# Mixer of an encoder block: v stores on the loading queue, one transfer for a q or k tile, earlier splits

## The chip, the cores and the metric

The kernel runs on one core of a Trainium2 chip. The metric is the time of one execution in microseconds (us) on the device; a kernel's time is the median of its runs. The core's engines are PE (TensorE, matrix products), ACT (ScalarE), DVE (VectorE), POOL (GpSimd) and SP (SyncE, which here only issues DMAs). DMAs are issued from the queues of SP (q1 in the profile), ACT (q10) and POOL (q0), and are carried out by the core's 16 DMA engines. Each engine works through its own instructions in order; a DMA issue is such an instruction too, so it waits in its engine's order for what its transfer needs.

## The reference

One layer of an encoder block, all in float32, with a sequence of 1024 tokens (a grid of 16 rows by 64 columns) and a model width of 1024:

```python
h = h + 0.5 * swiglu(rms_norm(h, ffn1_norm), ffn1_w_gate, ffn1_w_up, ffn1_w_down)
u = rms_norm(h, mix_norm)
z = u @ w_in                                  # columns: q | k | v | ssm input | gates
q, k, v, s_in, gates = jnp.split(z, [512, 1024, 1536, 2048], axis=-1)
y_attn = neighbourhood_attention(q, k, v, na_rpb) @ w_attn_out   # 8 heads of 64
y_ssm = s5_branch(s_in, ...) @ w_ssm_out
g_attn, g_ssm = jnp.split(jax.nn.sigmoid(gates), 2, axis=-1)
h = h + (g_attn * y_attn + g_ssm * y_ssm) @ w_out
h = h + 0.5 * swiglu(rms_norm(h, ffn2_norm), ffn2_w_gate, ffn2_w_up, ffn2_w_down)
h = h + (p @ w_ple_proj) * jax.nn.sigmoid(rms_norm(h, ple_norm) @ w_ple_gate)
return rms_norm(h, final_norm)
```

The attention of a token goes over a window of 8 rows by 16 columns around it, with a learned bias. The branch `s5_branch` runs 32 groups of diagonal complex state-space scans in both directions and ends with a gated unit:

```python
y = jax.nn.gelu(y)
y = y * jax.nn.sigmoid(y @ glu_w + glu_b)
```

## The kernel before

**Products.** Every operand of the products is split into a high and a low part of type float32r: `split` (L157 to L160) casts the high part on ACT (L159) and subtracts it on DVE for the low part (L160). `mm3` (L188 to L192) then makes three products: high by high, high by low, low by high. The projections from `u` (`w_in`) to q, k and the gates run as seven half-size products in place of eight (Strassen's scheme), in 128 x 512 blocks: for one pair of output blocks the items 0 to 6 are run by `s_run`; before an item runs, `s_load` has loaded the weight block `blk` (on ACT's queue), `s_prep` has added blocks where the scheme needs it and split the result into `wh` and `wl`, and `s_evac` takes the finished item from PSUM. `s_ahead(n)` loads five items ahead of n and splits one ahead; `s_more(n)` splits all items below n. A banked sum (`px`, `py`) must be copied out (`z`, on ACT) before PE may use its bank again.

**Order.** A generator `mixer_side` makes the work beside the projections: the state-space scans, the attention, and the gated unit. After every few products the main line calls `tick()`, which advances the generator; each `yield n` says how many ticks pass before its next piece. In this way PE's order is written out by hand. The order of ACT, DVE, POOL and SP in this part of the program is decided by a scheduler, which keeps data dependences and the rings of tile buffers.

**Values.** `values(t)` makes v for half of the sequence: 8 blocks by three products into four banks, then for each of 8 quarters a tile `vs` with high and low parts. The store of it to DRAM (`v_d`) is put into the list `later` with the queue that issues it, and `s_store` issues what is in the list. In `values(1)` the first q/k pair's weights are already being prepared. After it the kernel loads the four `s` tiles, from which further operands (`xh`, `xl`) for the projections are made.

**Attention.** 64 units: 8 heads by 4 column blocks (`cb`) by 2 row blocks (`rb`). Unit j makes its scores (`attn_scores`, L1243: `s<-khl,q`), two units later the transposes of the softmax (`attn_turn`, `pt`), another two later the product with v (`attn_values`, `O<-pth,vhl`). Between units PE runs projection products, in the fixed order. K and q lie in DRAM with high and low parts (`k_d` as [4, 2, 128, 1024]: head pair, part, 2 x 64 channels, token; `q_d` as [4, 128, 4, 2, 2, 128]: head pair, 2 x 64 channels, `cb`, then 512 numbers). A k tile holds the high part in partitions 0 to 63 and the low part in 64 to 127; a q tile holds the same 64 rows of `q_d` twice. `load_k` (L1210) is called for the next head in the fourth or sixth unit of a head, `load_q` (L1216) two column blocks ahead. Values are loaded likewise, by one DMA:

```python
vdr = v_d.rearrange("h (r c) d -> h r c d", r=4)
nc.sync.dma_start(hl[0:n].rearrange("p g d -> p (g d)").bitcast(F32), vdr[hd, :, KC0[cb]:KC0[cb] + KNC[cb]])
```

Its source has 4 outer parts, with 24 or 32 runs of 512 numbers in each; its target has 96 or 128 partitions.

**Gated unit.** `glu_load(m)` loads the two halves `yt` of output block m of the scan, `glu_act(m)` applies GELU to them in place on ACT, `glu_raw(k)` loads a weight block `wgs`. `glu_prep(t, k, raws)` splits the weight block into `wgl` and the operand into `yh` and `yl`, in the ring of buffers `tg`. `glu` runs 8 steps of 12 products, with the next step's `glu_prep` issued before each step's products; `part(11)` is the last of the projection pieces before it.

Of the kernel before, what the change touches and what calls it, by code (L numbers as in the profile page):

```python
# [8 lines left out]
F32 = mybir.dt.float32  # L9
F32R = mybir.dt.float32r  # L10
# [8 lines left out]
HT = 512  # L19
# [22 lines left out]
def encoder_block(ctx, tc, I, out):  # L42
# [119 lines left out]
    def ksl(k):  # L162
        return slice(k * P, (k + 1) * P)
# [910 lines left out]
    def part(n):  # L1074

        if "ac" in pools:
            pools.pop("ac").__exit__(None, None, None)
        if n:
            pools["ac"] = tc.tile_pool(name="as", bufs=1, reuse_waits="tile")
            pools["as"], pools["na"] = pools["ac"].__enter__(), n  # L1080
# [129 lines left out]
    def load_k(hd):  # L1210
        hp, i = hd // 2, hd % 2
        t = khl[hd] = ap_.tile([P, SEQ], F32R, tag="k4", bufs=2, name="khl")
        for a, s_ in enumerate(halves2):
            nc.sync.dma_start(t[s_].bitcast(F32), k_d[hp, a, halves2[i]])

    def load_q(hd, cb):  # L1216
        hp, i = hd // 2, hd % 2
        q = qs[hd, cb] = tmp("q", [P, 2, 2, P], F32R)
        for s_ in halves2:
            nc.sync.dma_start(q[s_].rearrange("p a t c -> p (a t c)").bitcast(F32),  # L1220
                              q_d[hp, halves2[i], cb].rearrange("p a t c -> p (a t c)"))

    def load_v(hd, cb):
        n = 4 * KNC[cb]
# [57 lines left out]
    def tg(name, shape=(P, HT), dt=F32):  # L1282
        return pools["as"].tile(list(shape), dt, tag="g", bufs=11, name=name)

    def glu_load(m, new=tmp):
        ygs[m] = [new("yt") for _ in range(2)]
        for i in range(2):
            nc.sync.dma_start(ygs[m][i], y_d[m, :, 4 * i:4 * i + 4].rearrange("p s c -> p (s c)"))
# [11 lines left out]
    def glu_raw(k, new=tg):  # L1300
        raw = new("wgs")
        nc.sync.dma_start(raw, I["wglu"][k])
        return raw

    def glu_prep(t, k, raws):
        w = ap_.tile([P, 2, HT], F32R, tag="k4", bufs=2, name="wgl")
        split(w[:, 0], w[:, 1], raws.pop(0))
        y = tg("yh", dt=F32R), tg("yl", dt=F32R)
        for src, hi, lo in glu_parts(t, k, *y):
            split(hi, lo, src)  # L1310
        if 4 * t + k < 6:
            raws.append(glu_raw((k + 2) % 4))
        return w, y

    def glu(raws):
        steps = [(t, k) for t in range(2) for k in range(4)]
        nxt = glu_prep(0, 0, raws)
        yield 3
        for n, (t, k) in enumerate(steps):
            w, y = nxt  # L1320
            if k == 0:
                os_ = [bank("glu") for _ in range(4)]
            if n in (1, 2):
                glu_act(n + 1)
            if k < 3:
                nxt = glu_prep(*steps[n + 1], raws)
            for m in range(4):
                mm3(os_[m], (w[:, 0, ksl(m)], w[:, 1, ksl(m)]), y, k == 0, k == 3)
            if k == 3:
                for m in range(4):  # L1330
                    sg = tg("sg")
                    A.activation(sg, os_[m], AF.Sigmoid, bias=glub[:, m:m + 1])
                    for src, o in glu_parts(t, m, sg):
                        V.tensor_tensor(o, o, src, ALU.mult)
                    nc.scalar.dma_start(y2_d[t, m], sg)
                    if m == 0 and t == 0:
                        nxt = glu_prep(1, 0, raws)
            yield 2 + k % 2
# [4 lines left out]
    def mixer_side():  # L1343
        yield from u_second()
        while 3 not in stored:
            yield 1
        yield 7
        new_x()
        ld = {}
        for pr in range(3):  # L1350
            ld[pr] = inject_load(pr)
        yield 10
        for pr in range(NPAIR):
            if pr + 3 < NPAIR:
                ld[pr + 3] = inject_load(pr + 3)
            inject(pr, *ld.pop(pr))
            yield 2
        while "v" not in stored:
            scan_steps(1)
            yield 1  # L1360
        part(5)
        for cb in range(4):
            scan_steps(4)
            yield 4
            if cb < 2:
                load_v(0, cb)
        load_tab(0)
        load_tab(1)
        while 0 not in ready:
            scan_steps(1)  # L1370
            yield 1
        units = [(hd, rb, cb) for hd in range(NH) for cb in range(4) for rb in range(2)]
        n = len(units)
        load_k(0)
        load_q(0, 0)
        load_q(0, 1)
        for _ in range(6):
            scan_steps(1)
            yield 2
        sms, pts, O = {}, {}, {}  # L1380
        late.clear()
        lo, so = {}, {}
        for j in range(n + 5):
            if j < n:
                hd, rb, cb = units[j]
                u = j % 8
                if rb == 1 and j // 2 + 2 < 4 * NH:
                    while u == 5 and hd + 1 not in ready:
                        yield 1
                    load_q(*divmod(j // 2 + 2, 4))  # L1390
                if u == 3 and hd + 1 in ready or u == 5 and hd + 1 < NH and hd + 1 not in khl:
                    load_k(hd + 1)
                if j and u in (0, 2, 6):
                    load_tab(3 * (j // 8) + (1, 0, 2, 0, 0, 0, 3)[u])
                sms[j] = attn_scores(hd, rb, cb)
            if 0 <= j - 2 < n:
                pts[j - 2] = attn_turn(units[j - 2][2], sms.pop(j - 2))
            while late:
                nc.scalar.dma_start(*late.pop())
            if 0 <= j - 4 < n:  # L1400
                hd, rb, cb = units[j - 4]
                if rb == 0:
                    O[0] = bank("O")
                attn_values(hd, rb, cb, O[0], pts.pop(j - 4))
                if rb == 0 and (j - 4) // 2 + 2 < 4 * NH:
                    load_v(*divmod((j - 4) // 2 + 2, 4))
            scan_steps(2)
            yield 3 + (j % 8 == 7)
        part(12)
        for p in range(3):  # L1410
            lo[p] = ssm_load(p)
        stored.add("scan")
        scan_steps(NCH)
        yield 4
        raws = []
        for p in range(NPAIR + 1):
            if 3 <= p + 3 < NPAIR:
                lo[p + 3] = ssm_load(p + 3)
            if p < NPAIR:
                so[p] = ssm_out(p, *lo.pop(p))  # L1420
            if p > 0:
                so.pop(p - 1)()
            if p in (6, 10):
                glu_load((p - 6) // 4)
            if p in (10, 14):
                glu_act((p - 10) // 4)
            if p == 11:
                raws.append(glu_raw(0, tmp))
            yield 1 + p % 2
        part(11)  # L1430
        raws.append(glu_raw(1))
        glu_load(2, tg)
        glu_load(3, tg)
        yield from glu(raws)

    start(mixer_side())

# [30 lines left out]
    def values(t):  # L1468
        os_ = [bank("v") for _ in range(4)]
        for k in range(NK):  # L1470
            load_wv()
            if t == 1 and k == 0:
                s_ahead(-2)
            if t == 1 and k == 2:
                s_store()
            if t == 1 and k == 5:
                s_ahead(0)
            wh, wl = Wv[k]
            xs = U[("a11", "a12", "a21", "a22")[2 * t + k // 4]][k % 4]
            for i in range(4):  # L1480
                xh, xl = (x[:, ksl(i)] for x in xs)
                T.matmul(os_[i], lhsT=xh, rhs=wh, start=(k == 0), stop=False)
                T.matmul(os_[i], lhsT=xh, rhs=wl, start=False, stop=False)
                T.matmul(os_[i], lhsT=xl, rhs=wh, start=False, stop=(k == NK - 1))
                tick()
        for i in range(4):
            for q in range(2):
                vs = tmp("vs", [P, 4, 2, 64], F32R)
                ov = os_[i][:, q * 256:(q + 1) * 256].rearrange("p (h d) -> p h d", h=4)
                with tc.high_priority(offset=PRI):  # L1490
                    A.copy(vs[:, :, 0], ov)
                    V.tensor_tensor(vs[:, :, 1], ov, vs[:, :, 0].bitcast(F32), ALU.subtract)
                later.append((nc.scalar, vds[ksl(i % 2), 2 * t + i // 2, 4 * q:4 * q + 4],
                              vs.rearrange("p h a d -> p h (a d)").bitcast(F32)))

    def load_br(t, b):
# [510 lines left out]
```

## Time and profile before

| what | us |
|---|---|
| median of 3 runs (lowest and highest) | 2094.0 (2091.51 to 2095.16) |
| the profiled execution, its own time | 2086.5 |
| its span, first to last instruction | 2084.6 |
| PE busy | 2045.0 |
| DVE busy | 1478.6 |
| ACT busy | 1012.6 |
| POOL busy | 481.2 |
| queue q1 (SP): MB moved; share of 16 DMA engines | 258.13; 39.0% |
| queue q10 (ACT): MB moved; share of 16 DMA engines | 49.32; 7.4% |

All rows but the first are of the profiled execution, which has its own time beside its span. The mixer lies between about 740 and 1200 us of the span. In rows of the profile `L1243` is line 1243 of the kernel; `s<-khl,q` reads "tile s made from tiles khl and q", buffer numbers left out; `x64` is a count. In a row of the timeline the first number is the start and the second the length, and the bracket at its end is the idle time before it and what ended it. In rows of waits the numbers are us in total, number, and longest. A share of 16 DMA engines adds up the time that a queue's packets took, over 16 times the length of the stretch. The mean granted clock of PE is 0.995 of full speed.

### The profile page before, as it was taken

The numbers are of one execution on the slowest core, as the hardware profiler recorded it, in microseconds if no ns is written. First come the engines' busy times: TensorE is split into PE (matmuls) and PEld (weight loads), VectorE is DVE, ScalarE is ACT, GpSimd is POOL, SyncE is SP. The second block draws the span as 40 slices with busy tenths as digits, with TensorE's granted clock in tenths as the row PEclk, the third lists the DMA queues.
The fourth block names the chain that finished last, engine by engine and source line by source line (L and its number), as shares of the span: only waits on it lengthen the run. The fifth ranks groups of instructions, "written<-read, shape, count | busy, mean of one in ns | idle before, by whom it ended". The sixth has DMA issues, their size and how long they took to land.

```text
span 2084.6 us, 27913 instructions
## 1 busy us (share of the span) xinstructions
PE 2045.0 (98%) x9326; PEld 1670.4 (80%) x9326; DVE 1478.6 (71%) x2542; ACT 1012.6 (49%) x1902; POOL 481.2 (23%) x700
## 2 busy tenths in 40 slices
PE   9999999999999999999999999999999999999998
PEld 3788888878888887877887888788888888888887
DVE  7897777667868755777745768986565666786855
ACT  6434333334445434767755646543333334445544
POOL 0037656441000508888331011000000000000000
PEclk9999999999999999999999999999999999999999
DMA  3434444476534466777684875243224238433302
GB/s 133 144 119 147 134 128 127 146 239 194 187 99 135 135 191 205 210 212 219 204 283 160 295 232 120 75 142 126 93 89 138 82 126 294 152 107 93 120 21 81
DMA packets 212592, 319.74 MB, mean 153 GB/s; under 512 B 29536, under 2 KB 79328, under 8 KB 212448
## 3 DMA queue, kind: packets, MB, share of 16 engines
q1 hardware_dynamic: 163216, 258.13, 39.0%
q10 hardware_dynamic: 44112, 49.32, 7.4%
q0 software_dynamic: 5120, 10.51, 2.0%
q8 instruction: 74, 1.21, 0.2%
q14 instruction: 70, 0.57, 0.1%
HBM read 224.01 MB, written 93.85 MB: 152 GB/s over the span
## 4 chain that ended last, share of the span: by engine, by line
PE 52%; DMA 4%; DVE 3%; ACT 2%; issue 1%; SPq 0%; ACTq 0%; DVEq 0%
PE dx L190 2%; PE dx L191 2%; PE dx L192 2%; PE ux L191 2%; PE gx L191 2%; PE ux L190 2%; PE gx L190 2%; PE gx L192 2%; PE ux L192 2%; PE br L192 1%; PE br L191 1%; PE br L190 1%; PE px L190 1%; PE px L192 1%; PE px L191 1%; PE dy L190 1%
## 5 line engine op out<-in xcount | busy, mean ns | idle before, releaser
L159 ACT CAST wh<-hbuf 128x512 fp32r<-128x512 f32 x280 | 172.9, 622 | 389.5 <-PE gx L191 84.7
L160 DVE TENSOR_TENSOR wl<-hbuf,wh 128x512 fp32r<-128x512 f32 x280 | 216.5, 776 | 121.3 <-ACT wh L159 119.2
L159 ACT CAST wh<-wblk 128x512 fp32r<-128x512 f32 x190 | 117.9, 622 | 188.8 <-PE dx L191 82.3
L160 DVE TENSOR_TENSOR wl<-wblk,wh 128x512 fp32r<-128x512 f32 x190 | 130.8, 691 | 50.3 <-ACT wh L159 42.7
L190 PE MATMUL dx<-ah,wh 128*128 128x512 f32 x416 | 163.5, 393 | 0.4 <-DVE hbuf L694 0.3
L192 PE MATMUL dx<-ah,wl 128*128 128x512 f32 x416 | 161.9, 389 | 0.0
L191 PE MATMUL dx<-al,wh 128*128 128x512 f32 x416 | 161.9, 389 | 0.0
L160 DVE TENSOR_TENSOR al<-araw,ah 128x512 fp32r<-128x512 f32 x154 | 106.6, 696 | 51.0 <-PE dx L191 21.1
L190 PE MATMUL gx<-xh,wh 128*128 128x512 f32 x320 | 125.1, 391 | 1.5 <-DVE c L581 1.5
L190 PE MATMUL ux<-xh,wh 128*128 128x512 f32 x320 | 125.1, 391 | 0.4 <-DVE c L581 0.4
L191 PE MATMUL gx<-xl,wh 128*128 128x512 f32 x320 | 124.5, 389 | 0.0
L192 PE MATMUL ux<-xh,wl 128*128 128x512 f32 x320 | 124.5, 389 | 0.0
L192 PE MATMUL gx<-xh,wl 128*128 128x512 f32 x320 | 124.5, 389 | 0.0
L191 PE MATMUL ux<-xl,wh 128*128 128x512 f32 x320 | 124.5, 389 | 0.0
L159 ACT CAST ah<-araw 128x512 fp32r<-128x512 f32 x154 | 95.0, 619 | 46.4 <-PE dx L191 14.2
L1167 POOL TENSOR_TENSOR sc<-X,rho 128x128 f32<-128x128 f32 x128 | 82.5, 645 | 59.5 <-ACT X L1150 49.6
L160 DVE TENSOR_TENSOR wl<-blk,wh 128x512 fp32r<-128x512 f32 x84 | 61.5, 732 | 46.9 <-ACT wh L159 43.6
L190 PEld LDWEIGHTS dx<-ah,wh 128*128 128x128 f32 x416 | 78.1, 188 | 18.6 <-DVE hbuf L694 1.2
L428 DVE TENSOR_TENSOR hbuf<-hbuf 128x512 f32<-128x512 f32 x120 | 90.3, 753 | 3.1 <-DMA hbuf<-in_wu 1.0
L191 PEld LDWEIGHTS dx<-al,wh 128*128 128x128 f32 x416 | 78.1, 188 | 16.7 <-issue 0.7
L192 PEld LDWEIGHTS dx<-ah,wl 128*128 128x128 f32 x416 | 78.1, 188 | 16.4
L190 PE MATMUL dy<-ah,wh 128*128 128x512 f32 x208 | 80.9, 389 | 0.0
(395 smaller groups left out, 5684.4 us busy)
## 6 DMA issues: line engine op xcount, KB each, us to landing
araw<-a_d SPq DMA_DIRECT2D x154, 256.0 KB
a_d<-c SPq DMA_DIRECT2D x148, 256.0 KB
wblk<-in_wd SPq DMA_DIRECT2D x88, 256.0 KB
hbuf<-in_wg SPq DMA_DIRECT2D x40, 512.0 KB
hbuf<-in_wu SPq DMA_DIRECT2D x40, 512.0 KB
blk<-in_win ACTq DMA_DIRECT2D x48, 256.0 KB
hbuf<-in_xT SPq DMA_DIRECT2D x32, 256.0 KB
h_d<-hbuf ACTq DMA_DIRECT2D x32, 256.0 KB
```

Of the source, the lines that this page charges most:

```text
L159: A.copy(hi, src)
L160: return eng.tensor_tensor(lo, src, hi.bitcast(F32), ALU.subtract)
L190: T.matmul(o, lhsT=wh, rhs=xh, start=first, stop=False, skip_group_check=more)
L191: T.matmul(o, lhsT=wh, rhs=xl, start=False, stop=False, skip_group_check=more)
L192: T.matmul(o, lhsT=wl, rhs=xh, start=False, stop=last, skip_group_check=more)
L428: V.tensor_tensor(b11, (b12, b22, None, None, b21)[i - 2], b11, ALU.subtract)
L1167: G.tensor_tensor(sc, both, rho4, ALU.mult)
```

## The change

- A k tile is loaded by one DMA to 128 partitions instead of two to 64; so is a q tile, whose source is read twice by a broadcast.
- The 16 stores of `v_d` are issued by SP's queue instead of ACT's.
- In `values(1)`, at its sixth block, the first q/k pair's items 1 and 2 are split as well (`s_more(2)`).
- The first `glu_prep` is made ahead of `part(11)`, in another ring of buffers (`tmp`); the loads behind it come in another order, and `glu` gives two ticks, not three, before its first products.

```diff
--- before.py
+++ after.py
@@ -1210,15 +1210,14 @@
     def load_k(hd):
         hp, i = hd // 2, hd % 2
         t = khl[hd] = ap_.tile([P, SEQ], F32R, tag="k4", bufs=2, name="khl")
-        for a, s_ in enumerate(halves2):
-            nc.sync.dma_start(t[s_].bitcast(F32), k_d[hp, a, halves2[i]])
+        nc.sync.dma_start(t.bitcast(F32), k_d[hp, :, halves2[i]])
 
     def load_q(hd, cb):
         hp, i = hd // 2, hd % 2
         q = qs[hd, cb] = tmp("q", [P, 2, 2, P], F32R)
-        for s_ in halves2:
-            nc.sync.dma_start(q[s_].rearrange("p a t c -> p (a t c)").bitcast(F32),
-                              q_d[hp, halves2[i], cb].rearrange("p a t c -> p (a t c)"))
+        src = q_d[hp, halves2[i], cb].rearrange("p a t c -> p (a t c)")
+        nc.sync.dma_start(q.rearrange("p a t c -> p (a t c)").bitcast(F32),
+                          src.unsqueeze(0).broadcast_to([2, 64, HT]))
 
     def load_v(hd, cb):
         n = 4 * KNC[cb]
@@ -1305,17 +1304,17 @@
     def glu_prep(t, k, raws):
         w = ap_.tile([P, 2, HT], F32R, tag="k4", bufs=2, name="wgl")
         split(w[:, 0], w[:, 1], raws.pop(0))
-        y = tg("yh", dt=F32R), tg("yl", dt=F32R)
+        new = tg if raws else tmp
+        y = new("yh", dt=F32R), new("yl", dt=F32R)
         for src, hi, lo in glu_parts(t, k, *y):
             split(hi, lo, src)
-        if 4 * t + k < 6:
+        if 4 * t + k < 6 and new is tg:
             raws.append(glu_raw((k + 2) % 4))
         return w, y
 
-    def glu(raws):
+    def glu(nxt, raws):
         steps = [(t, k) for t in range(2) for k in range(4)]
-        nxt = glu_prep(0, 0, raws)
-        yield 3
+        yield 2
         for n, (t, k) in enumerate(steps):
             w, y = nxt
             if k == 0:
@@ -1427,11 +1426,12 @@
             if p == 11:
                 raws.append(glu_raw(0, tmp))
             yield 1 + p % 2
+        nxt = glu_prep(0, 0, raws)
         part(11)
-        raws.append(glu_raw(1))
-        glu_load(2, tg)
-        glu_load(3, tg)
-        yield from glu(raws)
+        for k in (1, 2):
+            raws.append(glu_raw(k))
+            glu_load(k + 1, tg)
+        yield from glu(nxt, raws)
 
     start(mixer_side())
 
@@ -1475,6 +1475,7 @@
                 s_store()
             if t == 1 and k == 5:
                 s_ahead(0)
+                s_more(2)
             wh, wl = Wv[k]
             xs = U[("a11", "a12", "a21", "a22")[2 * t + k // 4]][k % 4]
             for i in range(4):
@@ -1490,7 +1491,7 @@
                 with tc.high_priority(offset=PRI):
                     A.copy(vs[:, :, 0], ov)
                     V.tensor_tensor(vs[:, :, 1], ov, vs[:, :, 0].bitcast(F32), ALU.subtract)
-                later.append((nc.scalar, vds[ksl(i % 2), 2 * t + i // 2, 4 * q:4 * q + 4],
+                later.append((nc.sync, vds[ksl(i % 2), 2 * t + i // 2, 4 * q:4 * q + 4],
                               vs.rearrange("p h a d -> p h (a d)").bitcast(F32)))
 
     def load_br(t, b):
```

The changed kernel is one line longer at its end, and its lines are shifted by one at most in this part. The rows below are of the order of instructions, before and after; no time is in them.

First SP, from the last loads of the scan's stage to the first loads of attention (`ut`, `fmi`, `tb`: loads for the scan and the bias tables; `s_...`: the four `s` tiles). Before:

```order
L1234 DMA tb<-in_tabs 128x768
L1632 DMA s_7141<-s_d 128x512
L1632 DMA s_7143<-s_d 128x512
L1632 DMA s_7145<-s_d 128x512
L1632 DMA s_7147<-s_d 128x512
L1226 DMA vhl<-v_d 96x1x512
L1226 DMA vhl<-v_d 128x1x512
L1214 DMA khl<-k_d 64x1024 x4
L1220 DMA q<-q_d 64x512 x6
L1234 DMA tb<-in_tabs 128x576
L1220 DMA q<-q_d 64x512 x2
```

And now:

```order
L1233 DMA tb<-in_tabs 128x768
L1592 DMA v_d<-vs 128x4x128 x7
L1633 DMA s_7146<-s_d 128x512
L1592 DMA v_d<-vs 128x4x128
L1633 DMA s_7148<-s_d 128x512
L1633 DMA s_7150<-s_d 128x512
L1633 DMA s_7152<-s_d 128x512
L1225 DMA vhl<-v_d 96x1x512
L1225 DMA vhl<-v_d 128x1x512
L1213 DMA khl<-k_d 128x1x1024 x2
L1219 DMA q<-q_d 128x1x512 x3
L1233 DMA tb<-in_tabs 128x576
```

The stores of v of the second half now stand on SP, seven of them ahead of the first `s` load, and the k and q loads have half the number and a target of the same form as that of `vhl`.

Second ACT, from the last copies of the scan's inputs (`X<-inj`) to the first copies `z` of the first q/k pair. Before:

```order
L1591 DMA v_d<-vs 128x4x128 x2
L1491 CAST vs<-v 128x4x64
L1591 DMA v_d<-vs 128x4x128 x2
L1545 DMA blk<-in_win 128x512
L159 CAST wh<-blk 128x512
L159 CAST xh<-s_7141 128x512
L159 CAST xh<-s_7143 128x512
L159 CAST xh<-s_7145 128x512
L159 CAST wh<-blk 128x512
L159 CAST xh<-s_7147 128x512
L1581 COPY z_7190<-px 128x512
```

And now:

```order
L159 CAST wh<-blk 128x512
L1150 COPY X<-inj 64x256 x2
L1136 DMA fmi<-f_d 128x256
L1150 COPY X<-inj 64x256 x9
L1492 CAST vs<-v 128x4x64 x8
L1546 DMA blk<-in_win 128x512
L159 CAST wh<-blk 128x512
L159 CAST xh<-s_7146 128x512
L1582 COPY z_7190<-px 128x512
```

The v stores are gone from ACT, and the cast of item 1's `wh`, which stood behind the weight load (`blk<-in_win`), now stands at the top of the second piece, among the scan's copies; the cast behind the weight load there is that of item 2.

Third ACT, around the start of the gated unit (`wgl`: its weights; `yh`: its operand; `ACTIVATE yt`: GELU; `wh`, `blk`, `z`: the projections). Before:

```order
L1581 COPY z_11100<-px 128x512
L1545 DMA blk<-in_win 128x512
L159 CAST wh<-blk 128x512
L159 CAST wgl<-wgs 128x512
L1545 DMA blk<-in_win 128x512
L1292 ACTIVATE yt<-yt 128x512
L159 CAST wh<-blk 128x512
L1292 ACTIVATE yt<-yt 128x512
L159 CAST wh<-blk 128x512
L159 CAST yh<-yt 128x256 x6
```

And now:

```order
L159 CAST yh<-yt 128x256 x2
L1582 COPY z_11060<-px 128x512
L1546 DMA blk<-in_win 128x512
L159 CAST wgl<-wgs 128x512
L159 CAST wh<-blk 128x512
L1291 ACTIVATE yt<-yt 128x512
L1546 DMA blk<-in_win 128x512
L1291 ACTIVATE yt<-yt 128x512
L159 CAST wh<-blk 128x512 x2
L159 CAST wgl<-wgs 128x512
L159 CAST yh<-yt 128x256 x4
```

The first step's `yh` moved ahead of both GELUs; those of the next steps stand behind them, two casts `wh` and a cast `wgl`.

## The prediction

> **What bounds the kernel now.** I read the page's totals first, then TensorE's waits between 740 and 1200 us (the mixer, where every edit lies), then stretches of time, then the DMA view of short windows.
>
> ```profile
> span 2084.6 us, 27913 instructions
> PE 2045.0 (98%) x9326; PEld 1670.4 (80%) x9326; DVE 1478.6 (71%) x2542; ACT 1012.6 (49%) x1902; POOL 481.2 (23%) x700
> ```
>
> TensorE (PE) is busy in 98% of the span, so all its idle time together is about 40 us. No edit touches a product, so a gain can come only out of that idle time and out of the lowered clock behind it. A loss has no such limit.
>
> ```profile
> PE pt L1259 <- ACT sm L1252: 7.5, 9, 1.6
> PE py L190 <- ACT wh L159: 4.6, 1, 4.6
> PE glu L190 <- ACT yh L159: 4.2, 1, 4.2
> PE py L192 <- DVE wl L160: 2.6, 1, 2.6
> ...
> PE s L1243 <- DMA q<-q_d: 0.5, 1, 0.5
> ```
>
> The columns are us in total, number, longest. The mixer's waits are two single stalls (4.6 us at the first q/k products `py`, 4.2 us at the gated unit), one of 2.6 us, and nine small ones in attention. Waiting for q is worth 0.5 us: today the q and k loads are hidden. The next rows (stretch, length, busy us by engine, granted clock, DMA share, GB/s) show the two stalls' aftermath and the whole attention stage, from the first k load to the last score product.
>
> ```profile
> 796.60:799.40 2.80, 2.79 (x7) 2.08 (x8) 2.80 (x4) 1.85 (x4) 2.49 (x5) 0.50 0.92 309
> 1105.40:1110.20 4.80, 4.76 (x11) 3.44 (x12) 4.03 (x9) 2.98 (x7) 0.00 (x0) 0.52 0.60 212
> 813.00:1040.00 227.00, 215.84 (x1148) 183.09 (x1147) 168.87 (x434) 160.99 (x378) 173.43 (x328) 0.99 0.74 216
> ```
>
> After each long stall the clock is near half: 2.8 x 0.50 = 1.4 us and 4.8 x 0.48 = 2.3 us more. In the attention stage the clock is 0.99, and the 16 DMA engines are busy 74% of 227 us. That figure is a mean over 16; the change alters how the load lies on single ones.
>
> **Part 1: one transfer for a q or k tile.** The number of DMAs falls by 40. Before, each transfer takes 64 rows of DRAM to 64 partitions. Afterwards the source's outermost dimension is 2 (`k_d[hp, :, ...]`; for q a broadcast of 2), ahead of 64 rows, and the target is 128 partitions. The kernel already has one load like this: `vhl<-v_d`, whose source has an outer dimension of 4 (`vdr[hd, :, ...]`), then 24 or 32 runs, onto 96 or 128 partitions. Two of them run almost alone in the trace. First their issue, then SP's queue (q1) in 800 to 802 us, and in 802 to 803.5 us, when a weight load on ACT's queue (q10) joins; last, 826 to 827 us, when only q tiles in the old form move (columns: packets, MB, share of 16 engines).
>
> ```profile
> 797.44 1.40 SPq L1226 DMA_DIRECT2D vhl<-v_d  x2
> ```
> ```profile
> q1 hardware_dynamic: 82, 0.17, 23.3%
> ```
> ```profile
> q10 hardware_dynamic: 97, 0.18, 40.9%
> q1 hardware_dynamic: 78, 0.15, 27.0%
> ```
> ```profile
> q1 hardware_dynamic: 144, 0.23, 92.1%
> ```
>
> Both `vhl` transfers are in flight and 12 engines have nothing else, yet the queue stays at 23 to 27%: four engines of 16, as many as the outer dimension says. The 64-row q loads fill 92%. So the new q and k loads should run on **two engines of 16**.
>
> [...]
>
> What that costs, from these rows and those of 813 to 1040 us:
>
> ```profile
> q1 hardware_dynamic: 13048, 26.65, 41.3%
> q10 hardware_dynamic: 21350, 22.13, 32.3%
> ...
> q<-q_d SPq DMA_DIRECT2D x64, 128.0 KB
> ...
> khl<-k_d SPq DMA_DIRECT2D x16, 256.0 KB
> vhl<-v_d SPq DMA_DIRECT2D x15, 256.0 KB
> vhl<-v_d SPq DMA_DIRECT2D x15, 192.0 KB
> ```
>
> - Speed of one engine: 0.17 MB in 23.3% x 16 x 2 us = 7.46 engine-us is 0.0228 MB per us.
> - q and k: 64 x 128 KB + 16 x 256 KB = 12.58 MB; on two engines 6.29 MB each, 6.29 / 0.0228 = 276 us.
> - `vhl`: 6720 KB = 6.88 MB on four engines, the busy two among them: 1.72 / 0.0228 = 75 us.
> - ACT's queue, spread over all: 32.3% of 227 = 73 us.
> - The rest of q1: 26.65 - 12.58 - 6.88 = 7.19 MB, a sixteenth each, at the queue's mean in this stage (26.65 MB in 41.3% x 16 x 227 = 1500 engine-us, 0.0178): 25 us.
>
> Sum: 449 us of work for each of the two engines, in a stage that PE fills in 227 us. They become the bound, and the stage grows by **222 us**. Ends: if packets of different queues pass side by side for nothing, only q and k count: 276 - 227 = +49 us. A window with a share over 100% (817 to 818 us) shows that some do overlap:
>
> ```profile
> q1 hardware_dynamic: 85, 0.28, 110.7%
> ```
>
> At the stage's mean speed for everything, 353 + 97 + 98 = 548 us, +321. I take +222: the `vhl` row is the nearest, being the same kind of load, queue and packet.
>
> Loading ahead doesn't hide this. A q tile now needs 0.262 / 0.0456 = 5.7 us of the pair, a k tile 11.5 us.
>
> ```profile
> L1214 SPq DMA_DIRECT2D khl<-k_d x16: 444/492/749, 813.2 to 990.7; - x16
> ```
> ```profile
> L1220 SPq DMA_DIRECT2D q<-q_d x64: 444/460/1474, 823.3 to 1024.5; - x64
> ```
> ```profile
> L1243 PE MATMUL s<-khl,q x128: 291/339/417, 827.7 to 1039.3; 128*128 128x288 f32 x64, 128*128 128x384 f32 x64
> ```
>
> Two k tiles issued from 813.2 us hold the pair until about 836, the first q tile is ready at about 842, and the first score product wants it at 827.7. After that a head (four q, one k) needs 34 us of the pair for q and k alone, while PE does a head in 212 / 8 = 26.5 us, so the lag grows from head to head. PE's small stalls in attention and its clock lie beneath this bound and are not counted again. What is queued behind the late loads waits too: `tb` and `vhl` behind them on SP, and the score products on PE, with all projection products that PE's fixed order has after them.
>
> **Part 2: v stores on SP, second operand earlier.** PE's first and second product group of the first q/k pair, then ACT's rows around the stall between them:
>
> ```profile
> 789.12 0.39 PE L190 MATMUL px<-xh,wh 128*128 128x512 f32 x1
> ...
> 796.61 0.80 PE L190 MATMUL py<-xh,wh 128*128 128x512 f32 x1 [4.61 <-ACT wh L159]
> ```
> ```profile
> 792.65 2.14 ACTq L1591 DMA_DIRECT2D v_d<-vs  x2
> 795.12 0.78 ACTq L1545 DMA_DIRECT2D blk<-in_win  x1
> 795.94 0.62 ACT L159 CAST wh<-blk 128x512 fp32r<-128x512 f32 x1 [3.00 <-DMA v_d<-vs]
> ```
>
> The cast `wh` for PE's second product group stood behind v stores and a weight load that waited for one. It is now cast among the scan's copies, well ahead of them, and ACT issues no v store: 4.6 + 1.4 = 6.0 us could go. But on SP the order puts seven v stores ahead of the first `s` load, and on ACT a cast of that tile now stands ahead of the copy `z` that frees PE's bank for the third group. The eight late stores are 2.1 MB; at 261 GB/s (next row) they end at about 797, so the tile lands near 797.5, cast and copy (0.62 + 0.58 us) end near 798.5, and the third group (without the stall due two groups of 12 products of 0.227 us after 789.1, at 794.6) waits 3 to 4 us, with the same half clock behind it.
>
> ```profile
> 789.00:792.00 3.00, 3.00 (x14) 2.15 (x12) 1.82 (x5) 1.30 (x4) 2.53 (x7) 1.00 0.93 261
> ```
>
> I take 1 us of gain; ends: 6.0 if the tile comes in time, 2 us of loss if the stores run a quarter slower beside ACT's weight loads (at 196 GB/s they end at 799.8). Nothing else waits on SP there, and POOL's order is unchanged.
>
> **Part 3: the gated unit.** The split of its first operand (`yh`) stood behind two GELUs that wait for loads:
>
> ```profile
> 1101.79 0.63 ACT L1292 ACTIVATE yt<-yt 128x512 f32<-128x512 f32 x1 [0.27 <-DMA yt<-y_d]
> ...
> 1103.64 0.63 ACT L1292 ACTIVATE yt<-yt 128x512 f32<-128x512 f32 x1 [0.71 <-DMA yt<-y_d]
> ...
> 1104.68 1.63 ACT L159 CAST yh<-yt 128x256 fp32r<-128x256 f32 x5
> ```
> ```profile
> 1105.44 0.80 PE L190 MATMUL glu<-yh,wgl 128*128 128x512 f32 x1 [4.21 <-ACT yh L159]
> ```
>
> Now it stands ahead of them, so step 0 starts without a wait (at 1105.4 - 4.2 = 1101.2, or three products of `part(11)` sooner, 1100.5): 4.2 + 2.3 = 6.5 us go. The second step's `yh` stays behind both GELUs and three casts after them; GELU end 1104.27 plus three casts of 0.6 is 1106.1, plus its own and the subtraction 1106.9, while step 1 is due 18 products of 0.227 us after 1100.5, at 1104.6: about 2.3 us come back, and some clock. I take 3.7 us; ends 0 (all of it comes back) and 6.5.
>
> Sum against the profiled execution: 2086.5 + 222 - 1 - 3.7 = 2303.8; its time lies 7.5 us under the median of 2094.0, so on that scale **2311 us**.
>
> **The rivals.**
>
> *Spread as before* (faster). If the target's 128 partitions set the spread, the loads use all 16 engines, and 40 fewer issues free ACT and SP in attention; of the waits there perhaps 2 us go (0 to 7.5, the row of nine). Then 2094 - 1 - 3.7 - 2 = 2087. It decides in `load_k` and `load_q` alone: were q1's share in a window of q loads near 90%, this would be it. Against it: `vhl` also has 96 or 128 partitions and keeps to 23%.
>
> *Two engines, but other two each time.* Then capacity isn't the bound, and only a tile's own 5.7 or 11.5 us counts. A k tile lands at about 825, in time; the first q tile, issued at 823.4, lands near 830 instead of before 827.7, later ones are issued two tiles (13 us) ahead. With 2 to 4 us lost and 4.7 gained: about 2092, between 2085 and 2100. Against it: two `vhl` transfers in flight would then fill 50%, not 23.3%.
>
> *The changes do what they say but are drowned*: parts 2 and 3 in full are worth 12.5 us, a twentieth of part 1; they can't turn its sign at any speed between its ends.
>
> **How the numbers follow.** Forecast 88%, spread as before 6%, other pairs 6%. The forecast's own ends are 2094 - 4.7 + 49 = 2138 and 2094 - 4.7 + 321 = 2410; they hold about nine in ten of its cases, so 2138 to 2415 holds 8 in 10 of all. Faster by over 0.2% (below 2089.8; about what a measurement can tell from no change): 6% and a little of the second rival, 7%. Same 3%. Slower 90%.
>
> **What would show it.** Right: in 813 us and after, PE waits for `q<-q_d` and `khl<-k_d` by over 100 us in all; the last score product near 1260 instead of 1039; the stage's DMA share near 0.4 with q1 near 12% where only q moves. Part 2: no `py` stall from `wh`, but one at a `px` from `z` near 795. Part 3: step 0 of `glu` starts right behind `part(11)`, step 1 waits about 2 us. It would be wrong if q1 reaches over half of the engines with q loads alone, or if PE's wait for q stays under 5 us.

## The result and the profile after

The changed kernel takes 2268.26 us (median of 4 runs, 2266.46 to 2269.53) against 2094.58 us before: a ratio of 1.083, 95% interval 1.0811 to 1.0848. The forecast was 2311 us, in a range of 2138 to 2415. The profiled execution took 2269.53 us, its span is 2267.8 us.

TensorE's waits from 740 to 1400 us in the changed kernel (us in total, number, longest):

```profile
PE s L1242 <- DMA q<-q_d: 98.0, 26, 14.2
PE pt L1258 <- ACT sm L1251: 21.2, 8, 8.0
PE px L190 <- ACT z L1582: 11.3, 4, 5.6
PE s L1242 <- issue: 9.8, 1, 9.8
PE px L192 <- DVE wl L160: 4.3, 1, 4.3
PE py L190 <- ACT z L1582: 3.6, 1, 3.6
PE glu L190 <- ACT yh L159: 2.3, 1, 2.3
```

Waiting for q rose from 0.5 to 98 us; it is the largest row by far. No row names a k tile. The stage that was 227 us long (813 to 1040) now lasts 406 us, from the first k load to the last score product:

```profile
L1213 SPq DMA_DIRECT2D khl<-k_d x8: 489/504/4309, 815.4 to 1134.9; - x8
```
```profile
L1242 PE MATMUL s<-khl,q x128: 291/341/687, 850.5 to 1220.8; 128*128 128x288 f32 x64, 128*128 128x384 f32 x64
```
```profile
815.00:1221.00 406.00, 263.10 (x1141) 212.57 (x1140) 170.45 (x434) 161.63 (x377) 150.34 (x323) 0.80 0.37 121
```

The last row is the stage in one line: the DMA share halved from 0.74 to 0.37 and the clock fell from 0.99 to 0.80, while 121 GB/s moved instead of 216. PE's idle time in the stage rose from 11 to 143 us (the length less the busy time), and the same products keep it busy 47 us longer at the lower clock. A mean of 37% looks like much room. It isn't, as two short windows show in which only SP's queue works: first 902 to 904 us, with PE idle throughout (its 0.00), and SP's queue in the DMA view of the same two us (27 packets, 0.10 MB: about 4 KB each, mostly a k tile); then both rows of 1214 to 1216 us (2 KB packets, a q tile).

```profile
902.00:904.00 2.00, 0.00 (x0) 0.00 (x0) 0.00 (x0) 0.00 (x0) 1.62 (x5) 1.00 0.13 52
```
```profile
q1 hardware_dynamic: 27, 0.10, 12.7%
```
```profile
1214.00:1216.00 2.00, 1.06 (x5) 1.08 (x6) 0.21 (x1) 0.00 (x0) 0.00 (x0) 0.50 0.13 50
```
```profile
q1 hardware_dynamic: 51, 0.10, 13.1%
```

Two engines of 16 are 12.5%: in these windows the other 14 carry next to nothing.

### The profile page after: what moved, and what is told of

Same layout as the page of the kernel before. It is cut to its first block, busy times and chain, and to the rows that moved or that the text cites. A ratio compares the mean times of both kernels' runs of the same rounds, so it can differ in the third digit from the quotient of the medians.

```text
span 2267.8 us, 27868 instructions
## 1 busy us (share of the span) xinstructions
PE 2092.2 (92%) x9326; PEld 1700.5 (75%) x9326; DVE 1480.1 (65%) x2542; ACT 1013.3 (45%) x1902; POOL 459.5 (20%) x700
## 4 chain that ended last, share of the span: by engine, by line
PE 74%; DMA 16%; DVE 5%; ACT 2%; issue 2%; POOL 1%; SPq 0%; ACTq 0%; DVEq 0%
DMA q<-q_d 8%; PE dx L190 4%; PE dx L191 4%; PE dx L192 4%; PE ux L190 3%; PE gx L190 3%; PE ux L191 3%; PE ux L192 3%; PE gx L192 3%; PE gx L191 3%; PE dy L191 2%; PE dy L192 2%; PE dy L190 2%; DMA khl<-k_d 2%; DMA tb<-in_tabs 2%
## 5 line engine op out<-in xcount | busy, mean ns | idle before, releaser
L1242 PE MATMUL s<-khl,q 128*128 128x288 f32 (+1 forms) x128 | 37.7, 380 | 109.1 <-DMA q<-q_d 98.0
L1242 PEld LDWEIGHTS s<-khl,q 128*128 128x128 f32 x128 | 25.7, 222 | 124.7 <-issue 102.8
L1246 DVE CUSTOM_DVE_ANT_0 sm<-s,tb 128x288 f32<-128x288 f32 (+1 forms) x64 | 32.2, 503 | 131.2 <-PE s L1242 82.8
L190 PE MATMUL px<-xh,wh 128*128 128x512 f32 x192 | 84.3, 439 | 11.3 <-ACT z L1582 11.3
```

Of the source, the lines that this page charges most:

```text
L190: T.matmul(o, lhsT=wh, rhs=xh, start=first, stop=False, skip_group_check=more)
L1242: T.matmul(s3, lhsT=qs[hd, cb][:, a, rb], rhs=kv, start=a == 0, stop=a == 1)
L1246: V.tensor_tensor_reduce(out=sm.rearrange("p (r c) -> p r c", c=n), in0=s3, in1=tab.rearrange("p (r c) -> p r c", c=n), scale=-1.0, scalar ...
```

## The experiments

All ratios below are against runs of the kernel before on the same chip. Experiments 1 to 4 shared one such set, 5 to 8 another, 9 to 11 a third (medians 2093.3, 2092.5 and 2092.5 us).

**1. Part 1 alone**, in the kernel before: only the diff of `load_k` and `load_q` that is shown in the change.

> The kernel before with part 1 alone (k and q in one transfer each, source's outermost dimension 2). Theory: two of 16 DMA engines carry these loads and bound attention, so nearly the whole loss is here: 2094 + 174 + about 5 for the missing parts 2 and 3, near 2273 us (2260 to 2285), last score product about 180 us later than before. Rival (the v stores on SP's queue delay the loads behind them): near 2094. Rival (both needed): in between.

Measured: 2265.81 us, ratio 1.0827 (1.0807 to 1.0848). The whole loss is part 1; v stores on SP's queue and the earlier splits are not needed for it.

**2. The change without part 1.**

```diff
-        nc.sync.dma_start(t.bitcast(F32), k_d[hp, :, halves2[i]])
+        for a, s_ in enumerate(halves2):
+            nc.sync.dma_start(t[s_].bitcast(F32), k_d[hp, a, halves2[i]])
...
+        for s_ in halves2:
+            nc.sync.dma_start(q[s_].rearrange("p a t c -> p (a t c)").bitcast(F32),
+                              q_d[hp, halves2[i], cb].rearrange("p a t c -> p (a t c)"))
```

> The changed kernel with q and k again in two transfers of 64 rows each; parts 2 and 3 stay. Theory: no loss is left, PE waits for q and k by under 2 us; the two moved parts gain about 4.7 us by their sums (1 at the first q/k pair, 3.7 at the gated unit), so 2088 to 2092 us. Rival (v stores on SP cost attention): above 2100.

Measured: 2090.89 us, ratio 0.9989 (0.9975 to 1.0002). No loss is left; whether parts 2 and 3 gain can't be told from no change.

**3. One transfer, rows outermost.** The number of DMAs, bytes and the target's 128 partitions stay as in the change; only the order of the source's dimensions is another: 64 rows, then 2, in place of 2, then 64.

```diff
-        nc.sync.dma_start(t.bitcast(F32), k_d[hp, :, halves2[i]])
+        nc.sync.dma_start(t.bitcast(F32), k_d[hp, :, halves2[i]].rearrange("a p s -> p a s"))
...
-                          src.unsqueeze(0).broadcast_to([2, 64, HT]))
+                          src.unsqueeze(1).broadcast_to([64, 2, HT]))
```

> The changed kernel with the same 40 single transfers, bytes, packets and targets of 128 partitions, but the source walked with the 64 channel rows outermost and the two parts (for q the two copies) inside them; the partitions of k and q are interleaved in the same way, so the scores sum the same products. Theory (the outermost dimension of the source decides how many DMA engines work): 64 spreads over 16 engines, the loss of 174 us is gone, 2084 to 2092 us. Rival (one large transfer instead of two small is slow in itself, by its length or because it holds a place among the DMAs in flight): near 2268. Rival (reading the same q rows twice is slow): half the loss or more stays.

Measured: 2081.06 us, ratio 0.9942 (0.9919 to 0.9965): 187 us less than the change, below the expected 2084 to 2092, and faster than the kernel before. SP's and ACT's queues from 827 to 1033 us of this kernel, then the last score product:

```profile
q1 hardware_dynamic: 12120, 25.60, 40.2%
q10 hardware_dynamic: 18819, 20.39, 31.1%
```
```profile
L1242 PE MATMUL s<-khl,q x128: 291/317/346, 830.7 to 1032.5; 128*128 128x288 f32 x64, 128*128 128x384 f32 x64
```

The share of q1 is back at 40%, and the score products last from 830.7 to 1032.5. That share is a mean; in 829 to 830 us, where only SP's queue works and its packets are those of q tiles, it fills over ten engines' worth:

```profile
q1 hardware_dynamic: 111, 0.20, 66.6%
```

This settles the mechanism: neither one large transfer nor the doubled reading of q rows is slow, since both are still there. The outermost dimension is what changed (and with it the order of the rows in the tile, for k and q alike).

**4 and 5. Only k, and only q, in one transfer** with the outer dimension 2; the other load is in two transfers of 64 rows.

> The changed kernel with only k in one transfer (outer dimension 2), q in two of 64 rows. Theory by capacity: the two engines get 92 us of k, 75 of vhl, 98 of the rest and 30 of q, 295 us, or 267 scaled by what the whole change measured against its sum (406 for 449), for a stage of 227: 2115 to 2160 us, and PE waits for k, not q. Rival (only q's broadcast is slow): 2088 to 2092, like the kernel without part 1.

> The changed kernel with only q in one transfer (outer dimension 2), k in two of 64 rows. Theory by capacity: the two engines get 184 us of q, 75 of vhl, 98 of the rest and 15 of k, 372 us, or 336 scaled by 406 for 449; 109 us over the stage's 227, so about 2200 us (2180 to 2240). Together with the 60 us of k alone this should come to about the 174 of both. Rival (the loss is a fixed wait per tile that comes too late, not capacity): k's 8 tiles cost 60, 32 q tiles of half the size would cost at least as much per tile, 7.5 us or 240 in all, above 2300.

Measured: k alone 2151.45 us, ratio 1.0278 (1.0252 to 1.0305); q alone 2206.5 us, ratio 1.0542 (1.0524 to 1.056). Against 2090.89 us of experiment 2, k costs 60.6 us, q 115.6, both together 177.4; 60.6 + 115.6 = 176.2, so the costs add. The capacity sums of the two expectations come to 40 and 109 us over the stage's 227, which is 149 and not the 179 of both; so the pair's total work alone does not give the measured costs. Per tile they are 7.6 and 3.6 us, as the tiles' sizes (512 and 256 KB) are; a fixed wait per tile is out. Per MB they are 14.4 us for 4.19 MB of k, 13.8 for 8.39 MB of q, 14.1 for both. With k alone PE waits like this:

```profile
PE s L1242 <- DMA q<-q_d: 23.0, 3, 9.8
PE px L190 <- ACT z L1582: 22.4, 2, 16.3
```

The first row shows that my expectation named the wrong tile: PE waits for q loads, not for k. The longest single wait is in the second row, 16.3 us for ACT's copy `z`. It is explained by two steps of the chain of work that ended last, in 815 to 860 us (start, length, what):

```profile
818.66 26.02 DMA khl<-k_d
844.75 0.34 ACTq L1546
```

By this chain the second of two k tiles took 26 us to land, and only then ACT issued its next weight load (L1546), which stands ahead of `z` in ACT's order. So a k tile delays ACT's work too, and not only what is behind it on SP's queue. k cost more than capacity says (60.6 us for 40); such waits are not in that sum, but how much of the difference they are was not measured.

**6. Rows outermost in the kernel before**, without parts 2 and 3 (edit of experiment 3 in the code of before).

> The kernel before with q and k in one transfer each, rows outermost (16 engines); v stores stay on ACT, no earlier splits. It tells what parts 2 and 3 are worth beside it. Theory (the 10 us between the two variants of the changed kernel come from attention alone, parts 2 and 3 give 2 to 3 us): 2082 to 2086 us. Rival (the gain needs the v stores off ACT's queue): 2090 or more.

Measured: 2078.46 us, ratio 0.9931 (0.9916 to 0.9947), below the expected 2082 to 2086. The gain of part 1 in this form needs no v stores off ACT's queue.

**7. Rows outermost, each tile in two transfers by columns**, in the changed kernel: as many DMAs as before.

```diff
+        for h in range(2):
+            nc.sync.dma_start(t[:, hsl(h)].bitcast(F32), k_d[hp, :, halves2[i], hsl(h)].rearrange("a p s -> p a s"))
...
+        for h in range(2):
+            nc.sync.dma_start(q.rearrange("p a t c -> p (a t c)")[:, h * 256:(h + 1) * 256].bitcast(F32),
+                              src[:, h * 256:(h + 1) * 256].unsqueeze(1).broadcast_to([64, 2, 256]))
```

> The changed kernel with rows outermost and 128 partitions, but each q and k tile in two transfers, split by columns: as many DMAs as before, spread over 16 engines. Theory (the 10 us come from 40 fewer issues that SP and ACT wait with): back to 2087 to 2092 us, attention stage about 212 us long. Rival (they come from the form of the target, 128 partitions in place of 64): 2079 to 2083 us, attention about 202.

Measured: 2082.58 us, ratio 0.9943 (0.9924 to 0.9962). My theory (40 fewer issues give the 10 us between experiments 2 and 3) falls: with the old number of DMAs the time stays that of experiment 3. The score products of this kernel, and below them those of experiment 2:

```profile
L1244 PE MATMUL s<-khl,q x128: 291/318/346, 829.2 to 1030.9; 128*128 128x288 f32 x64, 128*128 128x384 f32 x64
```
```profile
L1243 PE MATMUL s<-khl,q x128: 291/339/415, 829.6 to 1045.9; 128*128 128x288 f32 x64, 128*128 128x384 f32 x64
```

201.7 us against 216.3. The profiled execution of experiment 7 is 6 us faster than its median, but that of experiment 3, at its median, shows 201.8 as well. What is left as a cause, of what was varied here, is the form of a transfer: 128 partitions with the rows of both parts interleaved, instead of 64. It was not tried by itself in another place, and why 64 are slower stays open.

**8. Rows outermost, s loads on ACT, and the second step's `yh` sooner**, in the changed kernel.

```diff
-        nc.sync.dma_start(s3, s_d[k])
+        nc.scalar.dma_start(s3, s_d[k])
...
-        new = tg if raws else tmp
+        new = tmp if 4 * t + k < 2 else tg
...
-        if 4 * t + k < 6 and new is tg:
+        if 0 < 4 * t + k < 6:
```

> The changed kernel with rows outermost, the four s loads on ACT's queue instead of SP's (so not behind the v stores), and the second step's yh in the ring of the first one's. Theory: the px stall of 6.0 us behind z and its clock (1.4) go, as the s tile no longer waits for the seven v stores, and the gated unit's second-step stalls (2.4 and 0.9) go: 2068 to 2073 us. Rival (s tiles compete for the DMA engines with the same stores, whichever queue issues them): the px stall stays at 3 us or more, 2076 to 2079. Rival (an s load on ACT waits in ACT's order and delays the v casts): a stall in the v or first px products instead.

Measured: 2071.95 us, ratio 0.9901 (0.9885 to 0.9917). Both glu waits are gone from the list of waits. The px stall fell only from 6.0 to 3.9 us:

```profile
PE px L190 <- ACT z L1582: 3.9, 1, 3.9
```

So the queue was a part of that stall. The rest may be the transfers' competition with the v stores, as the first rival had it (a stall of 3 us or more); this was not tried by itself, and the time is not the rival's 2076 to 2079 but the theory's.

**9 to 11. Parts 2 and 3 one by one**, on the kernel of experiment 6: part 2 alone, part 3 alone, part 3 with the second step's `yh` as in experiment 8.

> The kernel before with rows outermost and part 2 alone (v stores on SP, second operand earlier). From the traces so far the py stall of 4.6 us is replaced by a px stall of 5.6 to 6.0 with the same clock behind it, so part 2 should cost about 1 to 2 us: 2079 to 2081, against 2078.5 without it. Rival (my forecast's gain of 1 us, or its end of 6): 2072 to 2078.

> The kernel before with rows outermost and part 3 alone (the gated unit's first operand sooner). The forecast's 3.7 us: 2074 to 2076. Rival (the second step's waits of 2.4 and 0.9 us, as the traces with part 3 show, leave 1 us at most): 2077 to 2079.

> As the last, with the second step's yh too in the ring of the first one's, so that it is cast ahead of the GELUs; part 2 is left out. Theory (both glu waits go: 4.1 us and 2.3 of clock): 2071 to 2073, as fast as the variant with s loads on ACT (2072) without any of part 2. Rival (the wait moves to a later step): 2075 to 2078.

Measured: 2079.8 us, ratio 0.9931 (0.9917 to 0.9946); 2077.02 us, 0.9926 (0.9911 to 0.9941); 2072.82 us, 0.9902 (0.9887 to 0.9917). Beside 0.9931 of experiment 6, part 2 is worth nothing that can be told, and neither is part 3 as it was made. With the second step's operand sooner as well, part 3 is worth about 0.3%, or 6 us (the intervals of experiments 6 and 11 just touch), and the kernel is as fast as experiment 8 without any of part 2. Experiments 8 and 11 are both faster than the kernel before by 1%.

## Why the prediction was right

**The mechanism.** The steps of part 1 held in the main: the spread follows the source's outermost dimension (12.7% and 13.1% in windows of k or q alone, beside the 12.5% that two of 16 engines are; 40.2% for the queue in the stage once 64 rows come first), the pair of engines holds up the stage, and the clock and PE's other stalls lie beneath it. That it is the same two engines each time is borne out by two k tiles in flight at once, which still fill only two (10.9%, and 12.8% with ACT's queue; "The start", below); the rival *two engines, but other two each time* asked for four there. Two of the signs were not met to the letter: PE's wait for q was 98.0 us, not over 100, and the last score product came at 1220.8 us, not near 1260.

**The rival that was too cheap.** *Spread as before* was wrong for this edit, but experiment 3 is that rival made true, and shows that its price was too small: 2087 forecast, 2081 measured. Its 2 us for attention should have been 10 to 14 (score products over 201.8 us instead of 211.6 before and 216.3 in experiment 2). I had counted freed issues there, and experiment 7 shows that they weren't it.

**The size.** 222 us forecast for the stage, 179 measured (406 against 227), 174 in the median. The step that was off is the speed of one engine. I took 0.0228 MB per us from a window of 2 us in which two `vhl` loads were just starting. The two windows above give more: 52 GB/s at 12.7% of 16 engines (2.03 engines) is 0.0256 MB per us for one engine with packets of about 4 KB, 50 GB/s at 13.1% (2.10 engines) is 0.0239 with packets of 2 KB. With these the 2.10 MB of k on each engine take 82 us and the 4.19 MB of q 175, which is 257 instead of 276 us; `vhl` takes 72 instead of 75. That term, here and in the sums of experiments 4 and 5, takes the pair to be among `vhl`'s four engines, which no run shows by itself; in 894 to 895 us of the changed kernel, with packets of 2 and 4 KB from k, q and `vhl` loads under way, SP's queue fills 25.6%, four engines' worth, where separate sets would allow six. With 70 for ACT's queue and the other 25 the sum is 424 instead of 449, beside 406 measured. So the engine's speed is 25 of the 43 us that the forecast was too high; where the other 18 went is not shown. That the sum comes so near is in part luck: with k alone the same kind of sum was 21 us too low (40 for 60.6). ACT's queue stood as forecast: 17.2% of 406 us = 70, for 73.

```profile
q1 hardware_dynamic: 11848, 26.64, 19.3%
q10 hardware_dynamic: 21414, 22.09, 17.2%
```

These are the two queues from 815 to 1221 us, with the bytes of before (26.65 and 22.13 MB).

**The start.** The first score product was forecast to wait until about 842 us; it came at 850.5, since the first q load was issued at 841.4 and not at 823.3. With k alone in one transfer it came at 850.3, with q alone at 835.8, so the k tiles delay it. The prediction let SP's loads and PE wait behind them, and counted ACT's queue only as 73 us of work spread over all engines. These are the two queues in 824 to 826 us, when both k tiles have been issued and neither has landed (the first lands near 830):

```profile
q1 hardware_dynamic: 22, 0.09, 10.9%
q10 hardware_dynamic: 23, 0.01, 1.9%
```

Together they fill 12.8%, two engines again, and ACT's queue moves one packet for each packet of k (23 and 22). (The prediction's row of 110.7%, which it took for overlap between queues, is of SP's queue alone; here the two queues take turns.) A weight load of ACT took 17 us here (first row, from the chain that ended last; 5.96 us for the one in that chain of the kernel before, at 837.35), and SP waited 18.8 us for stores of `q_d` on ACT's queue before it could issue q loads (810 to 870 us; in the kernel before 5.6 us in 805 to 850):

```profile
818.43 17.04 DMA blk<-in_win
```
```profile
SPq L1219 <- DMA q_d<-qkl: 18.8, 2, 11.0
```

So a transfer on two engines holds up the other queue as well, and through it the very loads that PE waits for.

**Part 2** came out on the other side of zero in this trace. The forecast of the mechanism was right, that of its size not. These are rows of ACT, SP and PE in the changed kernel:

```profile
795.87 0.62 ACT L159 CAST wh<-blk 128x512 fp32r<-128x512 f32 x1 [2.83 <-DMA v_d<-vs]
800.03 0.62 ACT L159 CAST xh<-s 128x512 fp32r<-128x512 f32 x1 [3.54 <-DMA s<-s_d]
800.55 0.58 ACT L1582 COPY z<-px 128x512 f32<-128x512 f32 x1
```
```profile
789.07 5.48 SPq L1592 DMA_DIRECT2D v_d<-vs  x7
794.74 0.69 SPq L1633 DMA_DIRECT2D s<-s_d  x1
```
```profile
801.18 0.80 PE L190 MATMUL px<-xh,wh 128*128 128x512 f32 x1 [5.57 <-ACT z L1582]
```
```profile
801.10:804.00 2.90, 2.82 (x7) 2.24 (x8) 2.68 (x5) 2.84 (x7) 2.66 (x4) 0.50 0.57 186
```

The py stall is gone, and the px stall that takes its place stands exactly where it was forecast: z behind the cast of an s tile, that behind the s load, that behind seven v stores. But the stall is 5.6 us and not 3 to 4. I let the s tile land with the stores' end at 797.5; its issue ended only at 795.4, and it landed near 800. So 1 us of gain became 1 us of loss (5.6 against 4.6, with the clock at 0.50 behind both, as the last row has it); experiment 9 against 6 can't tell that loss from nothing.

**Part 3** was too large. Step 0 starts without a wait, and step 1 waits 2.3 us for `yh`. The forecast had 2.3 us too, but up to the end of the subtraction; here that (`yl`) takes 1.1 us more, 3.4 in all. I also allowed too little for the clock, which fell after these stalls too (0.66 in the five us behind them, 1.7 us; the forecast left about 0.5 for it):

```profile
PE glu L191 <- DVE yl L160: 1.1, 1, 1.1
```
```profile
1292.00:1297.00 5.00, 5.00 (x16) 3.91 (x16) 3.21 (x8) 2.59 (x7) 0.00 (x0) 0.66 0.21 81
```

That is 4.2 + 2.3 us before against 2.3 + 1.1 + 1.7 after, 1.4 us of gain. It is too little to be told: experiment 10 against 6 shows no difference beyond the intervals.

## What to carry to other kernels

Before two transfers are merged into one, look at the outermost dimension of the merged access pattern, on the DRAM side too: here a 2 in that place put 12.6 MB on two of 16 engines and cost 174 us, and the same merge with the 64 rows outermost gained 10 us or more. A mean DMA share of 0.37 says nothing about the busiest engine; a window in which one queue works alone does (here 12.7% and 13.1% for two engines, 23.3% for the four of `vhl`). A load that already has the suspected form, here `vhl`, can be read in the trace before anything is built.

## What was unexpected of the hardware

Tiles of the same size in the same number of DMAs moved attention faster with 128 partitions per transfer (201.7 us of score products in experiment 7) than with 64 (216.3 in experiment 2). The cost of the two-engine loads was close to 14 us per MB whether k, q or both were so loaded, though the sums of capacity say that they should not add. While k tiles held the two engines, the packets of ACT's queue passed one for one with theirs (23 and 22 in 824 to 826 us), and both queues together filled 12.8% of the 16 engines: the others stood nearly idle.
